# The FFN down projection as seven products instead of eight: one level of Strassen's algorithm in a full-layer kernel

## The chip, the cores and the metric

The kernel runs on one core of one Trainium2 chip. The metric is the device time of one execution in microseconds. The kernel before was run three times: 1833.81, 1831.93 and 1827.96 us, median 1831.93. One further execution was recorded by the hardware profiler; all rows below are from that one. In the text, PE is the matrix engine (PEld its weight loads), DVE the vector engine, ACT the scalar engine, POOL the engine also called GpSimd, and SP the engine that here only issues DMAs.

## The reference

One layer over 1088 tokens (1024 prompt, 64 sample) of width 1024. Attention and an mLSTM branch come first; then the part that this case is about:

```
x = x + g1 * (merged @ w_out)
u2 = _rmsnorm(x, norm2_g) * (1 + sc2) + sh2
x = x + g2 * ((silu(u2 @ w_ff_gate) * (u2 @ w_ff_up)) @ w_ff_down)
y = _rmsnorm(x, final_g)
```

`w_ff_gate` and `w_ff_up` are 1024x2816, `w_ff_down` is 2816x1024, all fp32. The gain `g2` differs between the two groups of tokens. Call the gated product h (2816 features, 22 blocks of 128).

## The kernel before

Everything is feature-major: a tile holds 128 features by tokens, so a residual of width 1024 is 8 blocks of 128x1088. Each fp32 factor is split into a high and a low fp32r part, and one product is three matmuls (`mm3`, lines 76 to 78: high weight by high operand, high by low, low by high) into one PSUM accumulator. The split of a tile is a cast (ACT line 47, or POOL line 53) and a subtraction (DVE line 56, or POOL line 59).

The stages that the change touches, in order of time:

- **Output projection**, up to about 1071 us. The first token half is done block by block, then the second one in the loop `again`, which reloads five of the weight blocks and splits off their low part on POOL (`wl_wp`, line 59). POOL also adds up the squares for the second norm (`acc`, line 1104).
- **Gate and up projections**, about 1071 to 1545 us, in 32 jobs (`jobs`, `gate_up`). They already are a one-level Strassen form: seven products (order 1, 6, 5, 7, 2, 3, 4) on token quarters of 272, 12 matmuls of 128x272 each (line 1363), in four PSUM banks, with DVE and ACT combining the banks. Jobs 0 to 9 do the first ten hidden blocks for token half 0, jobs 10 to 21 do hidden blocks 10 to 21 for both halves, jobs 22 to 31 do the first ten again for half 1. Sums of weight quarters for the first ten blocks are made ahead, during attention, in DRAM (`wsum_d`): POOL issues DRAM-to-DRAM DMAs, a copy (line 172) and one that accumulates (line 170), and each is tied to its moment by a one-element DMA of SP into the same tile (line 166) on which it must wait. For the other twelve blocks POOL adds the weights on chip (`S`, lines 1306 to 1316). Each job ends with a store of its 128x544 piece of h to DRAM (`h_d`, line 1357).
- **Down projection**, from 1545 us on. `ffn_down` takes the hidden blocks in slices 10-13, 14-17, 18-21, 0-3, 4-7. For each slice it goes through the 8 output blocks m and three token chunks (320, 384, 384); a chunk takes 4 hidden blocks x 3 matmuls into one bank (`ps_fd`), and DVE then adds the bank times g2 into the residual accumulator `x1f` (`add_x1`, line 1439). The weights are loaded by SP and split on POOL (`wide_unit`, `wh_fd` and `wl_fd`); h is loaded back and split by ACT and DVE (`load_h`); POOL adds the residual (line 1460).
- **Last slice and final norm.** Hidden blocks 8 and 9 (`ps_fdl`) are done chunk by chunk, and behind each chunk come squares, their sum by matmul (`ps_ssy`), the reciprocal root, transposes (`ps_y`, line 1515) and the store of y.

The order on every engine is the order of the program text, rearranged by a scheduler; engines meet by semaphores. Tiles of a tag rotate through a fixed number of buffers, and a tile can only be written when the readers of its predecessor are done: raw, high and low weights have three buffers each, the pool `up` sixteen of 128x1088.

## Time and profile before

| | |
|---|---|
| median of three runs | 1831.93 us |
| lowest and highest run | 1827.96 and 1833.81 us |
| profiled execution, device time | 1832.56 us |
| its span in the trace | 1830.9 us |
| mean granted PE clock in it | 0.983 |
| PE busy | 1756.2 us, 96% of the span |

The profiled execution is 0.6 us above the median of the runs. About 1.7 us of its device time lie outside of the span of the trace. Times of day in the text (such as "1545 us") count from the start of the span. A row of a group of instructions gives line, engine, operation, output and inputs, shape, count, then busy time and the mean of one in ns, then idle time ahead of the group and who ended it. Matmuls overlap in their pipeline, so the mean of one is longer than the time from one start to the next.

### The profile page before, as it was taken

What the parts mean: (1) busy time and instruction counts of PE and PEld (TensorE: products, weight loads), DVE (VectorE), ACT (ScalarE), POOL (GpSimd) and SP (SyncE); (2) the same over time, 40 slices, a digit from 0 to 9 for tenths busy, and PEclk for the clock granted to TensorE, in tenths of its full rate; (3) what the DMA queues carried; (4) which work ended last, traced back from release to release, by engine and by line L of the source; (5) the groups of instructions that cost most, each with busy time, mean ns of one, the idle gap of its engine ahead of it and who ended that gap; (6) DMA issues with size and microseconds to landing.
All of it is one profiled execution on the core that took longest, in us unless ns stands there. A gap on an engine that the chain in (4) does not pass through costs nothing. (4 is left out here: it accounts for less than half of the span.)

```text
span 1830.9 us, 31719 instructions
## 1 busy us (share of the span) xinstructions
PE 1756.2 (96%) x12388; PEld 1691.3 (92%) x12388; DVE 1001.2 (55%) x1903; ACT 671.6 (37%) x1401; POOL 675.7 (37%) x554
## 2 busy tenths in 40 slices
...
GB/s 275 108 89 209 153 194 152 196 122 143 173 144 142 128 135 148 158 262 140 164 214 195 65 153 176 191 89 72 77 72 80 217 201 204 151 145 109 47 13 98
DMA packets 313208, 265.54 MB, mean 145 GB/s; under 512 B 13670, under 2 KB 285282, under 8 KB 313058
## 3 DMA queue, kind: packets, MB, share of 16 engines
...
q14 instruction: 52, 0.43, 0.1%
...
## 5 line engine op out<-in xcount | busy, mean ns | idle before, releaser
L76 PE MATMUL ps_fd<-hh,wh_fd 128*128 128x384 f32 (+1 forms) x480 | 157.1, 327 | 1.2 <-DVE hst L1355 1.2
L78 PE MATMUL ps_fd<-hh,wl_fd 128*128 128x384 f32 (+1 forms) x480 | 157.2, 327 | 0.0
L77 PE MATMUL ps_fd<-hl,wh_fd 128*128 128x384 f32 (+1 forms) x480 | 157.0, 327 | 0.0
L56 DVE TENSOR_TENSOR w<-wr,w 128x512 fp32r<-128x512 f32 x140 | 95.3, 691 | 38.9 <-ACT w L47 35.8
L1439 DVE SCALAR_TENSOR_TENSOR x1f<-ps_fd,mod,x1f 128x384 f32<-128x384 f32 (+2 forms) x128 | 60.4, 497 | 101.6 <-PE ps_fd L78 101.6
L47 ACT CAST w<-wr 128x512 fp32r<-128x512 f32 x140 | 85.2, 620 | 73.4 <-PE ps_gc L1363 24.7
L390 DVE TENSOR_TENSOR_SCAN re<-re 128x128 f32<-128x128 f32 (+3 forms) x64 | 102.3, 1600 | 15.0 <-ACT re L386 14.7
L53 POOL TENSOR_SCALAR wh_fd<-wr_fd 128x1024 fp32r<-128x1024 f32 x20 | 24.8, 1241 | 227.1 <-PE ps_ga L1363 119.4
L76 PEld LDWEIGHTS ps_fd<-hh,wh_fd 128*128 128x128 f32 x480 | 90.1, 188 | 1.4 <-POOL wl_fd L59 1.4
L78 PEld LDWEIGHTS ps_fd<-hh,wl_fd 128*128 128x128 f32 x480 | 90.1, 188 | 0.0
L77 PEld LDWEIGHTS ps_fd<-hl,wh_fd 128*128 128x128 f32 x480 | 90.1, 188 | 0.0
L47 ACT CAST hh<-hr 128x1088 fp32r<-128x1088 f32 (+1 forms) x26 | 24.0, 962 | 174.9 <-PE ps_fd L77 151.4
L1363 PE MATMUL ps_ga<-b1h,w 128*128 128x272 f32 x352 | 74.5, 291 | 2.9 <-ACT w L47 1.8
L386 ACT ACTIVATE re<-z 128x512 f32<-128x512 f32 (+2 forms) x96 | 47.4, 494 | 80.5 <-DVE z L382 66.0
L1363 PE MATMUL ps_gb<-b6h,w 128*128 128x272 f32 x352 | 75.1, 292 | 0.2 <-ACT g L1348 0.2
L1363 PE MATMUL ps_gd<-b7h,w 128*128 128x272 f32 x352 | 73.9, 289 | 0.0
L1363 PE MATMUL ps_gc<-b5h,w 128*128 128x272 f32 x352 | 73.8, 289 | 0.0
L1363 PE MATMUL ps_ga<-b2h,w 128*128 128x272 f32 x352 | 73.8, 289 | 0.0
L1363 PE MATMUL ps_gc<-b3h,w 128*128 128x272 f32 x352 | 73.7, 288 | 0.0
L1363 PE MATMUL ps_gd<-b4h,w 128*128 128x272 f32 x352 | 73.6, 289 | 0.0
L56 DVE TENSOR_TENSOR al<-ps_a,ah 128x512 fp32r<-128x512 f32 (+1 forms) x80 | 49.4, 629 | 32.0 <-ACT ah L47 31.7
L76 PE MATMUL ps_ga<-uh,wh_ga 128*128 128x384 f32 (+1 forms) x192 | 65.5, 341 | 0.4 <-DVE mod L227 0.4
...
## 6 DMA issues: line engine op xcount, KB each, us to landing
...
```

The source lines that it names most:

```text
L47: nc.scalar.copy(out, in_)
L53: nc.gpsimd.tensor_scalar(out, in_, 1.0, 0.0, ALU.mult, ALU.add)
L56: nc.vector.tensor_sub(out, in_, h.bitcast(F32))
L76: nc.tensor.matmul(ps, wh, xh, start=first, stop=False)
L77: nc.tensor.matmul(ps, wh, xl, start=False, stop=False)
L78: nc.tensor.matmul(ps, wl, xh, start=False, stop=last)
L386: nc.scalar.activation(rest[:, c0 : c0 + w], ps, AF.Sigmoid, scale=-scale)
L390: nc.vector.tensor_tensor_scan(r, r, r, 1.0, ALU.mult, ALU.bypass)
L1363: nc.tensor.matmul(ps, w[:, a, j, :], b[j // 2][:, j % 2, :], start=p in (1, 6, 5, 7) and j == 0 and k == 0, stop=j == 3 and k == 2, skip_ ...
L1439: nc.vector.scalar_tensor_tensor(x1[m][:, lo:hi], ps[:, lo - s : hi - s], mod[:, 40 + m, g : g + 1], x1[m][:, lo:hi], ALU.mult, ALU.add)
```

## The change

The down projection is cut in two along each of its three sides: hidden blocks into 11 even and 11 odd ones, outputs into m 0-3 and m 4-7, tokens into the first quarters of both halves (quarters 0 and 2) and the second ones (1 and 3). With one level of Strassen's algorithm in Winograd's form, seven products take the place of eight. Each product has 11 k-blocks, 4 output blocks and two pieces of 272 tokens, three matmuls each: 1848 matmuls of 128x272 in place of 1584 of 128x384 or 128x320. The order is 1, 2, 6, 5, 3, 7, 4 (`dn_seq`). Each product runs in two parts `mp` of two output blocks, that is in four banks, and the whole contraction stays in PSUM: products 2, 3 and 4 go on in the banks of 1, 5 and 7.

What feeds it:

- Four tables of weight sums in DRAM (`dsum_d`), in 16 steps of 1408 rows x 257 columns, with the same pair of DMAs as `wsum_d`: four in the loop `again`, one in each of jobs 10 to 21.
- Operand sums `tb_d` and `tc_d` (`t_job`): 22 times two loads of a 128x544 piece of h, four DVE additions of 128x272 and two stores, one at product 2 of each half-job from job 10 on while there are any, the last one behind the last job.
- Operands (`dn_operand`): 77 loads of 128x2x272, a cast on ACT and a subtraction on DVE, one `up` buffer for both parts. Weights (`dn_weights`): 14 times three groups of 4, 4 and 3 k-blocks by two output blocks; the cast is on ACT and the subtraction on DVE, so POOL has no part in the down projection any more.
- `x1f` is loaded from DRAM with the residual in it (8 loads of 128x1088). Product 1 is copied to `us` by ACT, product 6 is subtracted from it by DVE and goes to three of the four quarters of the output; the others are added as before.
- The final norm goes by token quarter (`finish`): quarter 1 behind the first part of product 4, quarters 3 and 0 within its second part, quarter 2 at the end.

```diff
+    def tied_sum(dst, edge, src, add, when):
+        nc.sync.dma_start(edge, when)
+        if add:
+            nc.gpsimd.dma_start(dst, src, accum_op=ALU.add)
+        else:
+            nc.gpsimd.dma_start(dst, src)
+    FP = FFB // 2
+    w4 = w_d.rearrange("(k two p) n -> two k p n", two=2, p=P)
+    dsum_d = {x: dram.tile([FP, P, 2, 257], F32, name=f"dsum{x}_d") for x in (1, 2, 3, 4)}
+    dsum_parts = {1: ((0, 512), (1, 512)), 2: ((0, 0), 1), 3: ((0, 0), (0, 512)), 4: ((1, 0), 2)}
+    dsum_todo = [(x, k, c) for x in (1, 2, 3, 4) for k in range(2) for c in range(2)]
+    def dsum_step(when):
+        if dsum_todo:
+            x, k, c = dsum_todo.pop(0)
+            src = dsum_parts[x][k]
+            if isinstance(src, int):
+                src = dsum_d[src][:, :, c, :]
+            else:
+                c0 = src[1] + 255 * c
+                src = w4[src[0], :, :, c0 : c0 + 257]
+            e = 0 if c else 256
+            tied_sum(dsum_d[x][:, :, c, :], dsum_d[x][0, 0:1, c, e : e + 1], src, k, when)
...
         sqs = wo_half(m, 1, ws, m == again[0], m == again[-1], some)
+        if m in again[1::2]:
+            dsum_step(x1v(m, HT, T)[0:1, 0:1])
...
                 nc.sync.dma_start(h_d[i][:, HT * h : HT * (h + 1)], hst)
+                if h == 0 and i >= NF:
+                    dsum_step(hst[0:1, 0:1])
...
+    def t_job(j, h):
+        r = slice(HT * h, HT * (h + 1))
+        b, c = (npl.tile([P, HT], F32, tag=t, name=f"f{t}{j}_{h}", bufs=1) for t in ("rr", "t2"))
+        nc.sync.dma_start(b, h_d[2 * j][:, r])
+        nc.sync.dma_start(c, h_d[2 * j + 1][:, r])
+        b0, b1, c0, c1 = b[:, :QT], b[:, QT:], c[:, :QT], c[:, QT:]
+        nc.vector.tensor_sub(b0, b0, b1)
+        nc.vector.tensor_sub(b1, c1, b1)
+        nc.vector.tensor_add(c1, c1, b0)
+        nc.vector.tensor_sub(c0, c1, c0)
+        nc.sync.dma_start(tb_d[j][:, r], b)
+        nc.sync.dma_start(tc_d[j][:, r], c)
+    dn = {}
+    def quarters(ap):
+        return ap.rearrange("p (h r t) -> p h r t", h=2, r=2)
+    def dn_operand(p, k, raw):
+        src, r = {1: (h_d[2 * k], 0), 2: (h_d[2 * k + 1], 0), 3: (h_d[2 * k + 1], 1), 5: (tb_d[k], 0),
+                  7: (tb_d[k], 1), 4: (tc_d[k], 0), 6: (tc_d[k], 1)}[p]
+        raw = raw.rearrange("p (h t) -> p h t", h=2)
+        oh, ol = (x.rearrange("p (h t) -> p h t", h=2) for x in
+                  (lambda t: (t[:, :HT], t[:, HT:]))(up.tile([P, T], F32R, tag="u", name=f"o{p}_{k}")))
+        nc.sync.dma_start(raw, quarters(src)[:, :, r])
+        hi_act(oh, raw)
+        lo_dve(ol, raw, oh)
+        dn[p, k] = oh, ol
+    dn_order = {p: list(range(FP)) for p in order}
+    dn_order[1] = list(range(NF // 2, FP)) + list(range(NF // 2))
+    def early_operands():
+        for k in dn_order[1]:
+            dn_operand(1, k, mtile(f"hr{k}", F32))
...
-            todo = chain([early_h(b) for b in slices[0]])
+            todo = early_operands()
         def hook(p, last):
             if last and raw:
                 nxt[p] = weight_op(nxt_i, p, raw)
-            if (k < NF and p in (6, 2)) or (k >= FFB and p == 5):
+            if (k < NF and p in (6, 2)) or (k >= FFB and p == 5) or (k == FFB and p == 6):
                 step(todo)
+            if k >= NF and p == 2 and sums_todo:
+                t_job(*sums_todo.pop(0))
...
+        if k >= NF and i % 2:
+            sums_todo += [(i // 2, h) for h in halves]
...
+    for x in sums_todo:
+        t_job(*x)
...
-    def ffn_down(blocks, first):
...
-                for c, (s, e) in enumerate(CHUNKS):
-                    ps = dbank(f"ps_fd{r0}_{m}_{c}")
-                    for j, i in enumerate(blocks):
-                        mm3(ps[:, : e - s], wh[:, j, mi, :], wl[:, j, mi, :], hh[i][:, s:e], hl[i][:, s:e], j == 0, j == nb - 1)
-                    add_x1(m, ps, s, e, first)
...
+    def evac(p, m, h, ps):
+        if p == 1:
+            nc.scalar.copy(us[m][:, h], ps)
+        elif p == 6:
+            nc.vector.tensor_sub(us[m][:, h], us[m][:, h], ps)
+            if h:
+                add_x1(m, None, 1, us[m])
+                add_x1(m + 4, None, 1, us[m])
+                for i in range(2):
+                    add_x1(m + 4, i, 0, us[m][:, i])
+        else:
+            m_, r = {2: (m, 0), 5: (m + 4, 1), 3: (m, 1), 7: (m + 4, 1), 4: (m + 4, 0)}[p]
+            add_x1(m_, h, r, ps)
+            if p == 4:
+                norm_step(m_, r, h)
+            elif p != 5 and h:
+                norm_step(m_, r)
...
+    def dn_weights(p, mp, ks):
+        def fills(raw):
+            raw, x = raw.rearrange("p (k b) n -> p k (b n)", b=2), 0
+            for ks_ in runs(ks):
+                k0, k1 = ks_[0], ks_[-1] + 1
+                if p in (1, 2, 4):
+                    c0 = 256 * mp + (512 if p == 4 else 0)
+                    src = w4[int(p != 1), k0:k1, :, c0 : c0 + 256]
+                else:
+                    src = dsum_d[{6: 2, 5: 1, 3: 4, 7: 3}[p]][k0:k1, :, mp, mp : mp + 256]
+                yield raw[:, x : x + k1 - k0, :], src.rearrange("k p n -> p k n")
+                x += k1 - k0
+        raw = wp.tile([P, KB, P], F32, tag="wr", name=f"wr_d{p}_{mp}_{ks[0]}")
+        for dst, src in fills(raw):
+            nc.sync.dma_start(dst, src)
+        wh, wl = (wp.tile([P, KB, P], F32R, tag=t, name=f"{t}_d{p}_{mp}_{ks[0]}") for t in ("wh", "wl"))
+        n = 2 * len(ks)
+        hi_act(wh[:, :n], raw[:, :n])
+        lo_dve(wl[:, :n], raw[:, :n], wh[:, :n])
+        return [x.rearrange("p (k b) n -> p k b n", b=2) for x in (wh, wl)]
...
+    def dn_mm(p, mp, mi, h, w, j, k):
+        (wh, wl), (oh, ol), ps = w, dn[p, k], banks5[mp, mi, h]
+        ks = dn_order[p]
+        for i, (a, b) in enumerate(((wh, oh), (wh, ol), (wl, oh))):
+            nc.tensor.matmul(ps, a[:, j, mi, :], b[:, h], start=p in (1, 6, 5, 7) and k == ks[0] and i == 0,
+                             stop=k == ks[-1] and i == 2, skip_group_check=True)
...
+    dn_seq = (1, 2, 6, 5, 3, 7, 4)
+    for x, p in enumerate(dn_seq):
+        ks = dn_order[p]
+        groups = [ks[0:4], ks[4:8], ks[8:]]
+        coming = [] if p == 4 else [(dn_seq[x + 1], k) for k in dn_order[dn_seq[x + 1]]]
+        def prepare(n):
+            for p_, k in coming[:n]:
+                dn_operand(p_, k, dn_raw(f"hr{p_}_{k}"))
+            del coming[:n]
+        prepare(16 - FP)
+        for mp in range(2):
+            if p == 1 and mp:
+                for m in range(KB):
+                    nc.sync.dma_start(x1[m], x1_d[m])
+            if p in (1, 6, 5, 7):
+                for h in range(2):
+                    for mi in range(2):
+                        banks5[mp, mi, h] = pbank(mp, f"ps_d{p}_{mp}_{mi}_{h}")[:, :QT]
+            if p < 4 or p > 4:
+                for ks_ in groups:
+                    w = dn_weights(p, mp, ks_)
+                    for j, k in enumerate(ks_):
+                        for mi in range(2):
+                            for h in range(2):
+                                dn_mm(p, mp, mi, h, w, j, k)
+                        if mp:
+                            prepare(1)
+                for mi in range(2):
+                    for h in range(2):
+                        evac(p, 2 * mp + mi, h, banks5[mp, mi, h])
             else:
+                ws = [dn_weights(p, mp, ks_) for ks_ in groups]
+                for h in range(2):
+                    for mis in ((0, 1),) if (mp, h) != (1, 1) else ((0,), (1,)):
+                        for w, ks_ in zip(ws, groups):
+                            for j, k in enumerate(ks_):
+                                for mi in mis:
+                                    dn_mm(p, mp, mi, h, w, j, k)
+                        for mi in mis:
+                            evac(p, 2 * mp + mi, h, banks5[mp, mi, h])
+                    if mp == 0 and h == 1:
+                        finish(1, 0)
+                    elif mp and h == 0:
+                        finish(3, 0)
+                        finish(0, 0)
+    finish(2, 1)```

Where it moves work, three places. **PE at the start of the down projection**, before (`ps_fd` with output block and chunk, `hh` and `hl` the parts of h):

```order
L76 MATMUL ps_fd_0_0_17276<-hh_15934,wh_fd_0_17271 128x320 [waits DVE_49,Pool_49]
L77 MATMUL ps_fd_0_0_17276<-hl_15935,wh_fd_0_17271 128x320
L78 MATMUL ps_fd_0_0_17276<-hh_15934,wl_fd_0_17272 128x320 [waits Pool_49]
L76 MATMUL ps_fd_0_0_17276<-hh_16216,wh_fd_0_17271 128x320
L77 MATMUL ps_fd_0_0_17276<-hl_16217,wh_fd_0_17271 128x320
```

and now (`ps_d` with part, output block in it and token half; `o_5` the operand of k-block 5, both of its parts in one tile):

```order
L1580 MATMUL ps_d_0_0_0_17557<-o_5_16107,wh_d_0_5_17563 128x272 [waits DVE_49,Activation_49]
L1580 MATMUL ps_d_0_0_0_17557<-o_5_16107,wh_d_0_5_17563 128x272
L1580 MATMUL ps_d_0_0_0_17557<-o_5_16107,wl_d_0_5_17564 128x272
L1580 MATMUL ps_d_0_0_1_17559<-o_5_16107,wh_d_0_5_17563 128x272 x2
L1580 MATMUL ps_d_0_0_1_17559<-o_5_16107,wl_d_0_5_17564 128x272
```

One accumulator stays with one bank for all 11 k-blocks, PE goes round four banks per k-block, and it waits for ACT and DVE where it waited for POOL.

**SP between the last job and the second product.** In the kernel before, the last store of h stands behind the weights of the next slices:

```order
L1357 DMA h_d<-hst_1_17007 128x544 [waits DVE_49]
L64 DMA wr_fd_3_17551<-in_w_ff_down 128x4x256 [waits DMAHW3_49,Pool_49]
L64 DMA wr_fd_0_17645<-in_w_ff_down 128x4x256 [waits DMAHW4_49,Pool_49]
L1357 DMA h_d<-hst_1_17132 128x544 [waits DMAHW1_49,DVE_49]
L64 DMA wr_fd_1_17737<-in_w_ff_down 128x4x256 [waits DMAHW5_49,DMAHW2_49,Pool_49]
```

Now, from the last store of h on (`ft` is the second load of the last `t_job`, `hr` the raw operands of product 2):

```order
L1385 DMA h_d<-hst_1_17390 128x544 [waits DVE_49]
L1404 DMA ft_1_17500<-h_d 128x544 [waits DMAHW4_49]
L1425 DMA hr_0_17532<-h_d 128x2x272 [waits DMAHW6_49]
L1425 DMA hr_1_17537<-h_d 128x2x272 [waits DMAHW7_49]
L1425 DMA hr_2_17542<-h_d 128x2x272 [waits DMAHW0_49,PE_49]
```

and the last of them ahead of the weights of product 2:

```order
L1425 DMA hr_10_17838<-h_d 128x2x272 [waits DMAHW2_49,DVE_49]
L1425 DMA hr_0_17913<-tc_d 128x2x272 [waits DMAHW3_49,DVE_49]
L1425 DMA hr_1_17918<-tc_d 128x2x272 [waits DMAHW4_49,DVE_49]
L1564 DMA wr_d_0_0_17938<-in_w_ff_down 128x4x256 [waits DMAHW5_49]
L1564 DMA wr_d_0_4_17992<-in_w_ff_down 128x4x256 [waits DMAHW6_49,DVE_49]
```

In between stand two stores of the `t_job`, eight loads of `x1f` and the other operands of product 2. The weights of product 2 now stand 25 rows behind the last store of h.

**POOL in the jobs with sums on chip.** Before, job 12 and the start of 13:

```order
L1306 TENSOR_TENSOR S_12_13362<-wr_u_13324 128x512 [waits DMAHW3_49]
L1313 TENSOR_TENSOR S_12_13398<-wr_g_13322,wr_u_13324 128x512 [waits DMAHW0_49,DVE_49]
L1307 TENSOR_TENSOR S_12_13363<-S_12_13362,wr_g_13322 128x512 [waits Pool_49]
L1316 TENSOR_TENSOR S_12_13436<-wr_g_13322,S_12_13363 128x512 [waits DVE_49,Pool_49]
L1306 TENSOR_TENSOR S_13_13603<-wr_u_13565 128x512 [waits DMAHW7_49]
```

and now:

```order
L1334 TENSOR_TENSOR S_12_13410<-wr_u_13372 128x512 [waits DMAHW5_49]
L1341 TENSOR_TENSOR S_12_13446<-wr_g_13370,wr_u_13372 128x512 [waits DMAHW6_49,DVE_49]
L1335 TENSOR_TENSOR S_12_13411<-S_12_13410,wr_g_13370 128x512 [waits Pool_49]
L177 DMA dsum_d<-in_w_ff_down 1408x1x257 [waits DMAHW1_49,DMASW5_49]
L1344 TENSOR_TENSOR S_12_13494<-wr_g_13370,S_12_13411 128x512 [waits DVE_49,Pool_49]
```

One DMA of the sums, which waits for SP's one-element DMA, stands ahead of the last weight sum of each such job.

200 lines of the change are left out of this document (73 added, 127 removed).

## The prediction

> **What bounds the kernel now.** I read the page's busy shares and its chain first, then the waits of PE from the output projection on, then the stretches of the last 800 us one by one.
>
> ```profile
> PE 1756.2 (96%) x12388; PEld 1691.3 (92%) x12388; DVE 1001.2 (55%) x1903; ACT 671.6 (37%) x1401; POOL 675.7 (37%) x554
> PE ps_ga L1363 7%; PE ps_gc L1363 7%; PE ps_gd L1363 7%; PE ps_fd L78 4%; PE ps_fd L76 4%; PE ps_fd L77 4%; PE ps_gb L1363 3%; PE ps_fdl L78 0%; PE ps_fdl L76 0%; PE ps_fdl L77 0%; DMA wr<-wsum_d 0%; DVE w L56 0%; DVE y L1524 0%; PE ps_ssy L1132 0%; PE ps_y L1515 0%
> ```
>
> PE is busy for 96%, and the chain's named parts are its matmuls, the down projection's (`ps_fd`) among them. In the part that the change touches, PE waits for next to nothing (waited for: total, times, longest):
>
> ```profile
> PE ps_ga L1363 <- ACT w L47: 1.8, 1, 1.8
> PE ps_fd L76 <- DVE hst L1355: 1.2, 1, 1.2
> PE ps_ga L1363 <- DVE x L1096: 1.1, 1, 1.1
> ```
>
> By stretch (columns: length, busy time of PE, PEld, DVE, ACT, POOL with counts, granted clock, DMA share, GB/s):
>
> ```profile
> 1023.00:1071.00 48.00, 47.43 (x368) 46.91 (x366) 39.80 (x49) 28.71 (x54) 25.03 (x17) 0.97 0.31 97
> 1071.00:1190.00 119.00, 116.48 (x912) 115.73 (x913) 94.92 (x180) 68.94 (x132) 6.87 (x5) 0.99 0.63 181
> 1190.00:1310.00 120.00, 120.00 (x957) 120.00 (x956) 60.77 (x120) 37.01 (x74) 29.81 (x24) 1.00 0.25 77
> 1436.00:1546.00 110.00, 108.84 (x867) 108.65 (x866) 76.19 (x144) 51.52 (x98) 8.99 (x6) 1.00 0.67 196
> 1546.00:1600.00 54.00, 54.00 (x329) 54.00 (x329) 29.96 (x43) 8.54 (x8) 18.88 (x9) 1.00 0.52 179
> 1546.00:1560.00 14.00, 14.00 (x88) 14.00 (x88) 7.91 (x11) 4.00 (x4) 3.64 (x2) 1.00 0.92 340
> 1786.00:1812.00 26.00, 26.00 (x179) 25.92 (x178) 16.25 (x38) 20.75 (x41) 15.33 (x17) 1.00 0.15 61
> 1812.00:1831.00 19.00, 8.90 (x68) 7.70 (x66) 9.74 (x27) 7.34 (x14) 3.40 (x5) 0.82 0.43 153
> ```
>
> From 1546 to 1812 us PE has no gap and its clock is whole: the time of the down projection is the time of its matmuls. So the first question is what a matmul costs, as a start-to-start distance. Three shapes (start, duration; the third with 12 per row):
>
> ```profile
> 1785.74 0.34 PE L78 MATMUL ps_fdl<-hh,wl_fdl 128*128 128x384 f32 x1
> ...
> 1787.86 0.34 PE L78 MATMUL ps_fdl<-hh,wl_fdl 128*128 128x384 f32 x1
> 1804.76 0.31 PE L76 MATMUL ps_fdl<-hh,wh_fdl 128*128 128x320 f32 x1
> ...
> 1805.49 0.31 PE L78 MATMUL ps_fdl<-hh,wl_fdl 128*128 128x320 f32 x1
> 1247.51 1.51 PE ps_gd L1363 x12
> 1249.02 1.51 PE ps_ga L1363 x12
> ```
>
> The first pair is 12 starts apart: 2.12/12 = 0.1767 us for 384 columns. The second is 5 apart: 0.73/5 = 0.146 (0.147 over a longer row of them) for 320. Twelve matmuls of 272 take 1.51: 0.1258. Per column that is 0.460, 0.459 and 0.462 ns, so the price is by columns, with nothing fixed worth naming. The 1190-1310 row confirms it (957 in 120 us: 0.1254).
>
> **The matmuls.** Before, counted from the text: 22 blocks x 8 outputs x 3 passes is 528 per chunk, so 1056 of 384 columns and 528 of 320: 1056 x 0.1767 + 528 x 0.147 = 186.6 + 77.6 = 264.2 us. The first and the last matmul of the stage, and some transposes between them:
>
> ```profile
> 1545.75 0.38 PE L76 MATMUL ps_fd<-hh,wh_fd 128*128 128x320 f32 x1 [1.16 <-DVE hst L1355]
> ...
> 1811.29 2.38 PE L1515 MATMUL ps_y<-ident,x1f 128*128 128x128 f32 x20
> ...
> 1818.23 0.31 PE L78 MATMUL ps_fdl<-hh,wl_fdl 128*128 128x320 f32 x1
> ```
>
> With the last one's own slot PE runs from 1545.8 to 1818.4, 272.6 us; the 8.4 beyond the matmuls are transposes and sums of squares. After: 1848 x 0.1257 = 232.3. A transpose costs 0.11 (2.1 us between the starts of 20); three of four token quarters, 72 transposes, now lie ahead of the last matmul, and some sums: 9. For 14 half products with a change of banks I add 1.5. Sum 242.8, or **29.8 less**.
>
> The Trainium skill, page "TensorE: Matmul & The Clock Gate", section "Back-to-back issue gap", speaks against this: it gives a sustained spacing of about 81 ns at 128 columns and 131 ns at 512 for a stream of weight loads and matmuls, so mostly a price per instruction. Interpolated (an estimate from that page), 272, 320 and 384 columns would cost 99.8, 106 and 114.3 ns, the old stage 176.7 us and the new one 184.4, a loss of 7.7. The trace disagrees: 125.8 against 176.7 ns is a ratio of 1.40, that of the columns 1.41. The trace decides; what such a price would do here by its rows is the first rival.
>
> **The tail.** From 1818.4 to the end of the span (1830.9) are 12.5 us: last addition, square, sums, root, scaling, store. The new tail has the same links for one quarter of 272 tokens instead of 320, without the step that ends POOL's and DVE's `acc`, but four banks instead of six make its last transposes wait for a read-out. I take -0.5 (from -2 to +1).
>
> **Feeding the new stage.** Unit costs by the nearest rows:
>
> ```profile
> L56 DVE TENSOR_TENSOR hl<-hr,hh 128x544 fp32r<-128x544 f32 x8 | 5.6, 721 | 0.6 <-ACT hh L47 0.6
> L47 ACT CAST hh<-hr 128x544 fp32r<-128x544 f32 x8 | 5.0, 644 | 1.7 <-DMA hr<-h_d 1.6
> L1356 DVE SCALAR_TENSOR_TENSOR hst<-hst,g 128x272 f32<-128x272 f32 x35 | 17.0, 486 | 0.4
> L47 ACT CAST wh_wp<-wr_wp 128x1024 fp32r<-128x1024 f32 x5 | 5.2, 1045 | 3.8 <-PE ps_wo L77 3.8
> ```
>
> A half product lasts 132 x 0.1257 = 16.6 us. In it ACT casts 11 x 256 weight columns (2.9 us by the last row) and on average 5.5 operands (3.5): 6.4. DVE subtracts the same (1.35 + 1.35 + 1.0, scaled from 721 ns per 544, and 4.0) and reads out four banks (4 x 0.49): 9.7. In product 6's read-out DVE has four subtractions and the additions of three quarters, about 7.5, so 15.2 of 16.6. SP moves 1.44 MB of weights and 1.5 MB of operands: 2.9 MB in 16.6 us are 177 GB/s, against 340 at a share of 0.92 in the 1546-1560 row. Three buffers let a group of weights be made two groups (10 to 12 us) ahead of its use. All of it fits beside PE: nothing, with a bound of 2.5 us per half product if DVE came late each time.
>
> **Transition: +2 (0 to 5).** Product 2's weights stand behind about 10 MB (product 2's operands 3.1, `x1f` 4.5, the rest stores, sums and these weights). SP can first issue them when the last store of h has landed, some 4.5 us after the last job; at the 340/0.92 = 370 GB/s that a full queue moves they arrive at about 31 us, with cast and subtraction 33; needed at 33.2. A tie, so I take 2.
>
> **Operand sums: +1 (0 to 6).** 88 DVE additions of about 0.44 to 0.49 us and 88 transfers of 272 KB. In jobs 10 to 21 DVE has 60.8 of 120 us, so 15 of the 22 lie there free. Seven remain for the last ten jobs (110 us): 7 x 4 x 0.45 = 13 us on DVE (76 of 110 before, less the old early slices), and SP waits in each for a store to land, a load, and DVE; behind it stand the next job's weights, which now arrive about a job ahead.
>
> **Weight sums: +2 (0 to 6).** The nearest rows are the sums of the other weights (minimum, median, maximum of an issue on POOL in ns; POOL's wait for the tie; time to landing):
>
> ```profile
> L170 POOL DMA_DIRECT2D wsum_d<-wsum_d x4: 1038/1060/1081, 262.5 to 373.2; - x4
> POOL wsum_d L170 <- DMA wsum_d<-cvo: 22.5, 4, 6.1
> DMA to landing us min/median/max: 9.4/10.8/14.6
> L59 POOL TENSOR_TENSOR wl_wp<-wr_wp,wh_wp 128x1024 fp32r<-128x1024 f32 x5 | 13.0, 2603 | 24.5 <-ACT wh_wp L47 24.5
> 262.00:285.00 23.00, 23.00 (x152) 23.00 (x151) 14.08 (x18) 6.95 (x14) 12.41 (x10) 1.00 0.86 173
> ```
>
> The new ones have 1408 rows instead of 512: an issue costs 1.1 us if it is by DMA, 2.9 if by row. In jobs 10 to 21 one stands ahead of a single weight sum that is needed half a job later: nothing; the cover is gone if the issue and its tie take over 7 us. The DMAs of these jobs (253 us: 24 half-jobs of 84 matmuls) come near a share of 0.9: 0.25 as in the 1190-1310 row, 12 x 10.8 us at 0.86 (0.44), and 15 operand sums of 1.1 MB at 370 GB/s (0.18). In `again` four issues with ties (2 to 6 us each) stand ahead of `wl_wp` blocks of 2.6 us, in a loop of 6 us per block where POOL is 25 of 48 busy: one or two may come late for PE, and first-job weights behind them. Two microseconds.
>
> **Sum:** 1832.6 - 29.8 - 0.5 + 2 + 1 + 2 = **1807.3**, so 1807 (25 under the median of the runs).
>
> **Rivals.** *A price per matmul.* If the mean durations (336 ns for 384 columns, 309, and 290 for 272) were what PE pays:
>
> ```profile
> L76 PE MATMUL ps_fd<-hh,wh_fd 128*128 128x384 f32 x320 | 107.6, 336 | 0.0
> L76 PE MATMUL ps_fd<-hh,wh_fd 128*128 128x320 f32 x160 | 49.4, 309 | 1.2 <-DVE hst L1355 1.2
> L1363 PE MATMUL ps_ga<-b1h,w 128*128 128x272 f32 x352 | 74.5, 291 | 2.9 <-ACT w L47 1.8
> ```
>
> 1848 x 0.290 against 1056 x 0.336 + 528 x 0.309 is 536 against 518: 18 slower, with the added terms 1855. The starts speak against it. *Preparation eats it.* If the sums keep the DMA engines near the 0.86 row through jobs 10 to 31, SP's loads come late by a microsecond each job, twice in the last ten: 12 + 20 with the terms above leaves about 1832, no change. For it: the last ten jobs already run at 0.67; against: weights come a job ahead and PE waits 1.8 us in all. *The new stage is bound by its feed* (the slower side): DVE makes the low part of every weight and operand and reads out every bank in order; where a half product's queue exceeds the 10 to 12 us of lead, PE stops, and the next half product starts with the debt. At 2.5 us for each of 14, 35: 1842. It decides once DVE's part goes from 9.7 over 16.6; only product 6 comes near.
>
> **How the numbers follow.** The forecast with its bounds (1800 with no added cost and the short tail, 1822 with all added costs near their upper ends) has 0.82; preparation eats it 0.09 (1822 to 1836); feed 0.06; price per matmul 0.03. Range 1800 to 1826. A measurement of this kernel tells about 0.3%, 5.5 us, from no change. Faster: 0.82 and 0.03 of the second case, 0.85; the same 0.06 of it; slower 0.09.
>
> **What would show it.** Right: matmuls of 128x272 in `ps_d` with 12 in 1.51 us; the stretch from the first `ps_d` to the last about 243 us with PE busy throughout but a gap below 5 us 33 us after its start; POOL empty in it. Wrong: waits of PE for ACT or DVE weights (`wl_d`) at each half product (feed), waits for `w` of DMA in jobs 22 to 31 or for `wl_wp` in the output projection (preparation), or starts farther apart than 0.126 (price). If the down stage starts over 10 us later than 1545.8, my terms for the sums were wrong.

## The result, and the profile after

The kernel got slower: 1901.59 us (four runs, 1896.52 to 1905.75) against 1832.87 (four runs, 1827.96 to 1836.01), a ratio of 1.0376 with a 95% interval of 1.0341 to 1.0411. I had forecast 1807, so 95 us were missing. The profiled execution took 1902.57 us, 1900.8 in its span, 69.9 more than before. Of ten runs of the kernel `onchip_spread4` further down one took 2865 us, at a granted clock of 0.633; it is left out of that kernel's ratio.

From the page of the kernel after: the busy shares, the chain by engine, and one of its costliest groups.

```profile
PE 1756.0 (92%) x12670; PEld 1682.2 (88%) x12670; DVE 1050.3 (55%) x2002; ACT 734.7 (39%) x1504; POOL 581.5 (31%) x497
...
PE 11%; DMA 2%; DVE 0%; ACT 0%; issue 0%; SPq 0%; DVEq 0%; ACTq 0%
...
L1393 PE MATMUL ps_gc<-b3h,w 128*128 128x272 f32 x352 | 81.5, 310 | 35.8 <-DVE hst L1371 35.7
```

PE is as busy as before in microseconds (1756.0 against 1756.2) although the down projection is shorter, and the gate and up matmuls of one bank (`ps_gc`) have 35.8 us of idle time ahead of them. In the kernel before, PE was idle for 3.7 us in that whole stage. Now the stretches of the kernel after, with the same columns as in the prediction: length, busy time of PE, PEld, DVE, ACT and POOL with counts, granted clock, DMA share, GB/s.

```profile
1071.00:1190.00 119.00, 103.36 (x757) 99.98 (x756) 78.94 (x154) 57.42 (x111) 6.80 (x6) 0.94 0.80 200
1190.00:1310.00 120.00, 108.39 (x813) 106.69 (x812) 71.93 (x137) 35.43 (x74) 32.00 (x23) 0.94 0.64 171
1310.00:1436.00 126.00, 106.00 (x787) 104.89 (x786) 62.84 (x122) 29.04 (x60) 33.30 (x24) 0.92 0.72 168
1436.00:1546.00 110.00, 100.42 (x756) 99.34 (x756) 63.50 (x125) 37.46 (x74) 17.14 (x13) 0.95 0.81 206
1546.00:1647.00 101.00, 88.08 (x673) 86.94 (x671) 65.90 (x134) 42.37 (x83) 0.00 (x0) 0.95 0.75 221
...
1647.00:1680.00 33.00, 32.89 (x253) 32.92 (x254) 13.15 (x19) 11.62 (x19) 0.00 (x0) 0.95 0.93 325
1680.00:1889.00 209.00, 207.84 (x1677) 206.79 (x1677) 125.26 (x218) 96.84 (x145) 0.00 (x0) 1.00 0.54 163
```

The down projection starts at 1647.1 instead of 1545.75 us, 101.3 late, and then does what was forecast: from there to 1889.8 us, 242.7 in all, PE has hardly a gap. Nearly all of the loss lies in the gate and up stage, whose first matmul starts 5.4 us late (1076.99 instead of 1071.55 us). From 1071 to 1647 us PE is idle for 576 - 506.3 = 69.7 us, against 3.7 in the same stage before, and its 3786 matmuls cost 506.3/3786 = 0.1337 us each against 0.1260, at a granted clock of 0.92 to 0.95 instead of 1.00. That is 66 us of gaps and 29 of slower matmuls; the remaining 6 are 46 matmuls more in the stretch, the end of the output projection, whose last matmul starts at 1076.36 instead of 1070.14 us.

Who holds PE, and who holds those? The longest waits of the kernel after in that stage and at its end (waited for: total, times, longest), for PE, then DVE, SP's queue and POOL (`frr` and `ft` are the two tiles that a `t_job` loads):

```profile
PE ps_gc L1393 <- DVE hst L1371: 35.7, 11, 9.9
PE ps_gd L1393 <- DVE hst L1373: 8.9, 3, 4.6
PE ps_ga L1393 <- ACT p L1366: 7.7, 3, 4.9
PE ps_d L1580 <- DVE hst L1383: 7.6, 1, 7.6
...
DVE frr L1406 <- DMA frr<-h_d: 66.7, 17, 11.3
DVE frr L1407 <- DMA ft<-h_d: 47.6, 19, 7.6
...
SPq L1404 <- DMA h_d<-hst: 57.8, 19, 11.1
SPq L1410 <- DVE frr L1407: 42.7, 15, 4.1
...
POOL dsum_d L175 <- DMA dsum_d<-hst: 41.7, 4, 20.0
```

Lines 1403 to 1411 are `t_job`. PE waits for bank read-outs (lines 1371 and 1373), which are short additions; DVE comes late to them because, in its order, a `t_job` stands ahead and waits for its two loads. SP stands in the same `t_job` (for a store of h to land before it loads that h back, and for DVE before it stores a sum), and behind it stand weight loads of the next job. And POOL waits for the tie of a weight sum. One stall shows the links, from the timeline of the kernel after (start, duration, engine, line, operation; in brackets the idle time before it and who ended it):

```profile
1407.95 1.91 POOL L175 DMA_DIRECT2D dsum_d<-in_w_ff_down  x1
...
1417.97 0.32 SPq L1403 DMA_DIRECT2D frr<-h_d  x1
...
1417.17 0.43 DVE L1369 TENSOR_TENSOR u<-p,ps_gb 128x272 f32<-128x272 f32 x1
1428.91 1.18 DVE L1406 TENSOR_TENSOR frr<-frr 128x272 f32<-128x272 f32 x1 [11.30 <-DMA frr<-h_d]
1430.02 0.43 DVE L1371 TENSOR_TENSOR hst<-ps_gc,u 128x272 f32<-128x272 f32 x1
...
1430.50 0.60 PE L1393 MATMUL ps_gc<-b3h,w 128*128 128x272 f32 x1 [9.87 <-DVE hst L1371]
1430.89 0.43 PE L1393 MATMUL ps_gc<-b3l,w 128*128 128x272 f32 x1
...
1433.16 0.43 PE L1393 MATMUL ps_gc<-b3h,w 128*128 128x272 f32 x1
```

POOL issues a weight sum at 1408. While it runs, SP issues a load of 272 KB that takes 10.9 us. DVE stands idle for 11.3 us; the read-out is behind that addition in its order and takes 0.43 us, and PE has waited 9.87 us for it. Then PE is slow as well: ten matmuls start in 1433.16 - 1430.89 = 2.27 us, 0.227 each instead of 0.1257. The Trainium skill, page "TensorE: Matmul & The Clock Gate", section "HAM oscillation — how this bites in real kernels", says that an idle stretch of PE beyond some 3.4 us brings its clock down and that the next work starts cold; the trace agrees, with a spacing 1.8 times the usual one behind this gap of 9.87 us. The granted clock is 0.50 from 1430.5 to 1435 us. The trace also shows that short gaps cost only themselves: of the gaps in this stage the seven of 3.8 to 9.9 us are each followed by ten matmuls 0.227 us apart or more, and the thirteen of 0.4 to 2.7 us by ten that are 0.125 to 0.127 apart; two of 3.4 and 3.7 us have slow and usual ones behind them. (One gap of 2.05 us in the kernel `no_wsums` below was followed by slow ones, though.)

How long that weight sum took, and what it cost the DMA engines, stands in the DMA view of the kernel after for 1400 to 1434 us (queue, packets, MB, share of the 16 engines; then the issue, its size, time to landing). q1 are SP's transfers, q0 POOL's:

```profile
q1 hardware_dynamic: 4181, 3.69, 38.0%
q0 software_dynamic: 2227, 1.61, 33.2%
...
dsum_d<-in_w_ff_down POOLq DMA_DIRECT2D x1, 1413.5 KB, 22.2
```

It landed after 22.2 us, and a MB of it takes 20.6% of the engines' time in the stretch where a MB of SP's loads and stores takes 10.3%.

### The profile page after: what moved, and what is told of

It reads as the page before. It is cut to its first block, busy times and chain, and to the rows that moved or that the text cites. A ratio compares the mean times of both kernels' runs of the same rounds, so it can differ in the third digit from the quotient of the medians.

```text
span 1900.8 us, 32728 instructions
## 1 busy us (share of the span) xinstructions
PE 1756.0 (92%) x12670; PEld 1682.2 (88%) x12670; DVE 1050.3 (55%) x2002; ACT 734.7 (39%) x1504; POOL 581.5 (31%) x497
## 3 DMA queue, kind: packets, MB, share of 16 engines
q1 hardware_dynamic: 340290, 267.03, 48.1%
q0 software_dynamic: 30208, 62.04, 15.9%
## 5 line engine op out<-in xcount | busy, mean ns | idle before, releaser
L1580 PE MATMUL ps_d<-o,wh_d 128*128 128x272 f32 x1232 | 232.6, 288 | 8.7 <-DVE hst L1383 7.6
L1580 PEld LDWEIGHTS ps_d<-o,wh_d 128*128 128x128 f32 x1232 | 194.1, 189 | 9.1 <-ACT g L1380 7.7
L1580 PE MATMUL ps_d<-o,wl_d 128*128 128x272 f32 x616 | 177.5, 289 | 0.0
L47 ACT CAST w<-wr 128x512 fp32r<-128x512 f32 x140 | 83.5, 618 | 91.0 <-DMA wr<-wsum_d 27.6
L1580 PEld LDWEIGHTS ps_d<-o,wl_d 128*128 128x128 f32 x616 | 116.3, 189 | 0.2 <-DVE wl_d L56 0.2
L1393 PE MATMUL ps_gc<-b3h,w 128*128 128x272 f32 x352 | 81.5, 310 | 35.8 <-DVE hst L1371 35.7
L1393 PEld LDWEIGHTS ps_gc<-b3h,w 128*128 128x128 f32 x352 | 63.0, 204 | 38.7 <-DVE hst L1371 38.6
L1393 PE MATMUL ps_gd<-b4h,w 128*128 128x272 f32 x352 | 81.6, 311 | 8.9 <-DVE hst L1373 8.9
L1393 PE MATMUL ps_ga<-b2h,w 128*128 128x272 f32 x352 | 75.6, 293 | 7.7 <-ACT p L1366 7.7
L1393 PE MATMUL ps_ga<-b1h,w 128*128 128x272 f32 x352 | 77.3, 296 | 2.4 <-ACT g L1376 2.1
L56 DVE TENSOR_TENSOR wl_d<-wr_d,wh_d 128x1024 fp32r<-128x1024 f32 (+1 forms) x42 | 47.6, 1135 | 54.4 <-ACT wh_d L47 53.9
L1393 PE MATMUL ps_gb<-b6h,w 128*128 128x272 f32 x352 | 75.4, 291 | 1.9 <-ACT w L47 1.8
L1393 PE MATMUL ps_gd<-b7h,w 128*128 128x272 f32 x352 | 75.3, 293 | 1.4 <-DVE hst L1383 1.4
L1393 PE MATMUL ps_gc<-b5h,w 128*128 128x272 f32 x352 | 74.6, 291 | 2.0 <-DVE g L1379 1.6
L47 ACT CAST o<-hr 128x544 fp32r<-128x544 f32 x77 | 49.5, 645 | 62.2 <-DMA hr<-h_d 44.3
L1393 PEld LDWEIGHTS ps_gd<-b4h,w 128*128 128x128 f32 x352 | 64.7, 210 | 9.8 <-DVE hst L1373 5.0
L47 ACT CAST wh_d<-wr_d 128x1024 fp32r<-128x1024 f32 (+1 forms) x42 | 41.1, 979 | 78.7 <-PE ps_d L1580 69.6
L56 DVE TENSOR_TENSOR o<-hr,o 128x544 fp32r<-128x544 f32 x77 | 54.4, 724 | 30.7 <-ACT o L47 30.2
L1393 PEld LDWEIGHTS ps_ga<-b2h,w 128*128 128x128 f32 x352 | 59.0, 191 | 8.7 <-ACT p L1366 8.4
## 6 DMA issues: line engine op xcount, KB each, us to landing
dsum_d<-in_w_ff_down POOLq DMA_DIRECT2D x12, 1413.5 KB, 13.7
```

Source lines behind the costliest of these rows:

```text
L47: nc.scalar.copy(out, in_)
L56: nc.vector.tensor_sub(out, in_, h.bitcast(F32))
L1393: nc.tensor.matmul(ps, w[:, a, j, :], b[j // 2][:, j % 2, :], start=p in (1, 6, 5, 7) and j == 0 and k == 0, stop=j == 3 and k == 2, skip_ ...
L1580: nc.tensor.matmul(ps, a[:, j, mi, :], b[:, h], start=p in (1, 6, 5, 7) and k == ks[0] and i == 0, stop=k == ks[-1] and i == 2, skip_group ...
```

## The experiments

All times are set beside a kernel before of 1832.7 to 1835.4 us, measured in the same batch. Since the loss builds up in the gate and up stage, one table follows it through all kernels: how many us later than in the kernel before a half-job begins (the start of ACT's copy of its first bank; second job, job 10, job 22), and how much later the down projection does. A kernel that leaves work out is marked with *. The times are single runs, or medians of four where a ratio is given (ten for `onchip_spread4`); the lags are from the one profiled execution of each kernel.

| kernel | job 1 | job 10 | job 22 | down | time, us |
|---|---|---|---|---|---|
| after | 23.2 | 29.5 | 75.9 | 101.3 | 1901.59 |
| neither * | 0.2 | -0.3 | -0.3 | -0.4 | 1797.66 |
| no_opsums * | 17.5 | 17.4 | 22.4 | 30.7 | 1828.84 |
| no_wsums * | -0.7 | 7.0 | 12.6 | 35.9 | 1837.68 |
| pool_adds | 17.2 | 28.5 | 73.0 | 95.6 | 1896.93 |
| early | 92.8 | 99.4 | 107.3 | 128.3 | 1931.32 |
| early_poolq | 92.4 | 93.2 | 95.1 | 100.5 | 1902.53 |
| early_keep | 96.3 | 95.3 | 95.9 | 99.9 | 1898.43 |
| keep | 21.6 | 22.5 | 63.9 | 80.9 | 1881.32 |
| spread4 | 14.9 | 15.3 | 57.0 | 72.4 | 1869.43 |
| spread8 | 26.8 | 26.6 | 60.7 | 62.8 | 1864.91 |
| onchip | 29.0 | 28.7 | 40.5 | 52.1 | 1851.73 |
| onchip16 | 10.4 | 10.5 | 51.8 | 62.3 | 1859.63 |
| onchip_no_wsums * | 1.6 | 2.4 | 7.8 | 9.4 | 1808.88 |
| onchip8 | 3.4 | 4.0 | 53.7 | 55.7 | 1857.40 |
| onchip_half * | 2.5 | 2.9 | 17.7 | 19.9 | 1819.30 |
| onchip_spread4 | 10.2 | 10.8 | 21.9 | 33.5 | 1835.76 |

A lag can be there before anything that was added runs. The first matmul of the output projection starts at 950.68 us in the kernel before, at 954.08 in `after`, 948.16 in `no_opsums`, 953.29 in `keep`, 959.56 in `onchip` and 958.25 in `onchip16`, and none of these has an added instruction ahead of it. So a lag, and the time of a single run, can be off by up to about 10 us; what a stage adds to the lag is the safer number.

### One half of the preparation at a time

Two causes were to be told apart first: waits for the loads of `t_job` in the order of an engine (theory A), and DMA engines filled by the weight sums (theory B). `no_opsums` takes out the operand sums, `no_wsums` the weight sums, `neither` both:

```diff
# no_opsums, neither
     def t_job(j, h):
+        return
...
-        src, r = {..., 5: (tb_d[k], 0), 7: (tb_d[k], 1), 4: (tc_d[k], 0), 6: (tc_d[k], 1)}[p]
+        src, r = {..., 5: (h_d[2 * k], 0), 7: (h_d[2 * k], 1), 4: (h_d[2 * k + 1], 0), 6: (h_d[2 * k + 1], 1)}[p]
# no_wsums, neither
-        if dsum_todo:
+        if False:
...
-                    src = dsum_d[{6: 2, 5: 1, 3: 4, 7: 3}[p]][k0:k1, :, mp, mp : mp + 256]
+                    src = w4[0, k0:k1, :, 256 * mp : 256 * mp + 256]
```

> The 22 operand sums (loads, DVE additions, stores) are left out; products 5, 7, 4 and 6 read h itself in the place of the sums, so their operands are not the right ones, but every transfer and matmul of the down projection stays. In the changed kernel the lag behind the kernel before grows by 22 us up to the first job's end, by 12 in jobs 1 to 9, by 44 in jobs 10 to 21 and by 23 in jobs 22 to 31, and the down projection itself takes the 242 us forecast. Theory A (DVE works in order and waits for the loads of the operand sums, ahead of the bank read-outs that PE waits for): the 79 us of jobs 1 to 31 go, the first 22 stay, about 1823 us (1815 to 1835). Theory B (the weight sums crowd the DMA engines, everything else comes late): little changes, over 1875 us.

> The 16 steps of weight sums are left out; products 6, 5, 3 and 7 load a quarter of the weights themselves in the place of a sum, so the result is not the reference's, but the loads of the down projection are as many and as large. Theory A: only the 22 us up to the first job go (four steps stand in the output projection there), and loads land a little earlier, about 1870 us (1855 to 1882). Theory B: DMA engines are free, the waits for the operand sums' loads shrink to nothing, about 1825 us (1805 to 1840).

> Both the weight sums and the operand sums are left out (operands and weights of the dependent products are read from h and from the weights themselves, so the result is not the reference's). Both theories: what is left is the new down projection on its own, 1832.6 - 30.3 + 2 = 1804 us (1800 to 1810), with the down stage at 242 to 244 us. If the time is over 1820, a third cause lies in the down stage's transition.

With neither, 1797.66: the new down stage by itself gains 35 us, and no half-job is late. The weight sums alone bring that to 1828.84 (31 more), the operand sums alone to 1837.68 (40 more), both to 1901.59 (104 more). So either alone eats the gain, and 33 us come only from the two together (27, if what each kernel had lost or won before its output projection is taken off). The first run came out as theory A had it, the second as theory B, so neither theory holds alone. The table says where the two meet: between jobs 10 and 22 the weight sums alone add 5 us to the lag, the operand sums alone 6, and both together 46. Two stretches of `neither`, one in jobs 10 to 21 and one at the start of the down stage:

```profile
1190.00:1310.00 120.00, 120.00 (x957) 120.00 (x956) 60.50 (x119) 37.30 (x74) 30.04 (x24) 1.00 0.25 77
...
1546.00:1680.00 134.00, 134.00 (x1079) 134.00 (x1078) 81.21 (x124) 60.95 (x89) 0.00 (x0) 1.00 0.74 236
```

The gate and up stage is as before, to the count of its matmuls, and the new stage runs without a gap at 134/1079 = 0.1242 us per matmul.

What the weight sums do alone: in `no_opsums` 16 of the 31 us are lost between the first job and the second. Its stretch of 1085 to 1105 us, and ACT's waits around it:

```profile
1085.00:1105.00 20.00, 14.01 (x95) 13.27 (x93) 10.13 (x20) 5.80 (x11) 0.00 (x0) 0.91 1.01 196
```

```profile
ACT w L47 <- DMA wr<-in_w_ff_up: 9.4, 1, 9.4
ACT w L47 <- DMA wr<-wsum_d: 8.1, 4, 3.5
```

The DMA engines are full (1.01), and ACT waits for the first jobs' weights: the four steps of the loop `again` run while these are loaded. After that the single steps of jobs 10 to 21 cost 5 us, and the last ten jobs 8.

What the operand sums do alone: in `no_wsums` they cost 8 us in the first ten jobs, 6 in jobs 10 to 21 and 23 in the last ten. DVE's waits for the loads, and PE's for the read-out of line 1371, in `no_wsums`:

```profile
DVE frr L1407 <- DMA ft<-h_d: 58.6, 20, 7.9
DVE frr L1406 <- DMA frr<-h_d: 45.4, 18, 5.3
...
PE ps_gc L1393 <- DVE hst L1371: 3.6, 4, 1.3
```

DVE waits 104 us in all, hardly less than the 114 of the kernel after, but no wait is longer than 7.9 us where the longest there was 11.3, and PE waits 3.6 us for that read-out where it waited 35.7. So the sum of DVE's waits does not tell what they cost; with the weight sums beside them the single waits got longer, and PE ran dry.

### Which engine's order

`pool_adds` moves the 88 additions to POOL, so that DVE no longer waits for the loads:

```diff
-        nc.vector.tensor_sub(b0, b0, b1)
+        nc.gpsimd.tensor_sub(b0, b0, b1)
   (and the three additions behind it)
```

> The 88 additions of the operand sums are done by POOL instead of DVE; all transfers are as in the changed kernel. Theory A: DVE no longer waits for these loads, POOL does; PE's waits for the bank read-outs on DVE (46 us in the changed kernel) go, some come back through the weight sums of jobs 10 to 21 that POOL makes on chip behind them; about 1855 us (1830 to 1875). Theory B: the same transfers are as late as before, 1890 to 1910 us.

1896.93: no gain to speak of, and within what theory B expected. The waits of `pool_adds`, of SP, ACT and PE:

```profile
SPq L1404 <- DMA h_d<-hst: 68.4, 20, 6.7
SPq L1410 <- POOL frr L1407: 63.3, 21, 4.3
...
ACT w L47 <- POOL S L1344: 73.5, 11, 15.6
...
PE ps_ga L1393 <- ACT p L1366: 26.2, 8, 8.6
```

The stall has moved, not gone. Now POOL waits for the same loads ahead of its weight sums `S`, ACT waits for those (73.5 us), and PE for ACT. That DVE alone was the cause is refuted. The waits fit a wider reading, that it matters little which engine on the way to PE waits in its order for a load that comes late; this run doesn't part that from theory B.

The next three move all 16 weight-sum steps into the attention stage, where earlier sums of this kind already are; `early_poolq` also puts the loads, additions and stores of `t_job` on POOL's queue, and `early_keep` takes most of the operand sums from tiles that are still on chip:

```diff
# early: one step behind each of 16 units of attention
-        if m in again[1::2]:
-            dsum_step(x1v(m, HT, T)[0:1, 0:1])
...
-                if h == 0 and i >= NF:
-                    dsum_step(hst[0:1, 0:1])
...
+                fill += [ads[x], dsum_unit(16 + ai - na + x)]
# early_poolq: the same, and in t_job nc.vector and nc.sync -> nc.gpsimd
# early_keep: the same, and for half 1 and all of blocks 10 to 21, in short:
-        nc.sync.dma_start(c, h_d[2 * j + 1][:, r])
+        b = kept_h[2 * j] if j < NF // 2 else even[h]   # c is hst itself, even[h] is loaded
```

> All 16 steps of weight sums are moved into the attention stage (one behind each of 16 units of its filler work); nothing else changes. Without these steps the changed kernel took 1837.7 us. Theory C (what costs time is SP's order: an issue that waits for a store to land or for DVE holds up every later load and store, and the DRAM-to-DRAM sums lengthen each landing) and theory D (the volume of all transfers together crowds the DMA engines) both say 1838 to 1848: the 31 us of the weight sums and the 33 that both together cost go, the 40 of the operand sums stay.

> As the run with early weight sums, and the operand sums are wholly POOL's: it issues their 88 transfers on its own queue and does the 88 additions. The transfers are as many and as large. Theory C: SP and DVE no longer wait for any of it; what is left is POOL being late with the weight sums of jobs 10 to 21, 1800 to 1818 us. Theory D: as many bytes at the same times, 1835 to 1850 us.

> As the run with early weight sums, and the operand sums are made at the end of each odd job: its own h is taken from the tile on chip, the even block's is loaded at the start of the odd job (jobs 10 to 21, stored long before) or also taken from the chip (jobs 22 to 31); five pairs of the first ten blocks are still loaded both, in even jobs. 61 transfers of 272 KB instead of 88, and no load waits for a store just issued. Theory C: 1799 to 1810 us, faster than the kernel before by 1.2 to 1.8%. Theory D: 30% fewer bytes give 30% of the 40 us back, about 1828 us.

`early` took 1931.32, `early_poolq` 1902.53 and `early_keep` 1898.43 (ratio 1.0346, 1.0328 to 1.0364), all three far outside what I expected, and for a reason that I had not priced: the attention stage has no room either. Two stretches there, of `early` and of the kernel before:

```profile
600.00:700.00 100.00, 69.77 (x491) 63.80 (x489) 45.75 (x88) 31.20 (x73) 26.22 (x27) 0.86 0.86 184
700.00:800.00 100.00, 66.62 (x437) 59.60 (x427) 45.59 (x90) 27.55 (x65) 24.25 (x22) 0.81 0.83 174
```

```profile
600.00:700.00 100.00, 94.66 (x673) 85.81 (x672) 66.89 (x132) 45.26 (x106) 25.74 (x28) 0.97 0.59 144
700.00:800.00 100.00, 91.96 (x685) 81.86 (x683) 77.12 (x151) 47.00 (x110) 39.99 (x42) 0.98 0.66 170
```

The DMA share goes from 0.59 and 0.66 to 0.86 and 0.83, and about a third of PE's matmuls in these stretches is pushed out (928 where there were 1358). The first gate and up job is 91 us late.

But these three tell something else apart. Once the jobs run, what do the operand sums cost with no weight sum beside them? From the first job (lags of 91.3, 90.9 and 94.8 us) to the down projection `early` grows later by 37 us, `early_poolq` by 9.6, `early_keep` by 5.1. `early` and `early_poolq` move the same bytes in the same stage, only in another queue; so in that stage, and with no weight sum beside them, it is the order on SP and DVE that costs 27 us, not the volume.

### Operand sums from tiles on chip

`keep` is the change with only the operand sums of `early_keep`; `spread4` and `spread8` also put four or eight of the weight-sum steps into attention, and the rest singly into jobs 10 to 21 or 10 to 17:

```diff
# spread4; spread8: (18, 21, 24, 27, 30, 32, 34, 36) and range(10, 18)
-        if m in again[1::2]:
-            dsum_step(x1v(m, HT, T)[0:1, 0:1])
...
-                if h == 0 and i >= NF:
+                if h == 0 and i in range(10, 22):
...
+                fill += ads[x : x + 1] + [dsum_unit(n)] * (n in (20, 25, 30, 36))
```

> The changed kernel with only the operand sums rearranged: made at the end of each odd job from its tile on chip, the even block's piece loaded early or also taken from the chip. The weight sums are where the change has them. Theory C (SP's and DVE's order; the weight sums lengthen the landings on which they wait): with the waits gone, what both cost together beyond each alone (33 us) and most of the 40 go; the weight sums' own 31 and some 4 stay: 1797.7 + 35 = 1833 us (1826 to 1842). If the two only compete for the DMA engines (theory D), 1850 to 1880.

> As the run before it, and the four weight-sum steps of the output projection are moved into the attention stage, far apart (one per 60 to 100 us); the twelve others stay in jobs 10 to 21. With weight sums alone the lag was 16 us at the first job, nothing up to job 24 and 13 from there on; the first 16 should go: 1797.7 + 4 + 13 + 2 = 1817 us (1805 to 1825), faster than the kernel before by 0.5 to 1.5%.

> As the last, with eight steps in the attention stage (one per 35 to 45 us) and eight in jobs 10 to 17. If the 13 us around jobs 22 to 25 came from the last steps running into the next stage's loads, they go too. If the attention stage has no room for more transfers (16 steps at one per 19 us cost 95 us there), it loses 5 to 25 us instead. 1797.7 + 4 + 5 to 25: 1807 to 1827, I take 1814.

Measured 1881.32, 1869.43 and 1864.91 (the last two are 1.0189 and 1.0173 times the kernel before, with intervals of 1.017 to 1.0207 and 1.0128 to 1.0218). Each gains, all three far less than I expected. In `keep` the loads that are left are where the time goes: pairs of the first ten blocks (line 1432) and the even ones of the other twelve (line 1369). DVE's waits in `keep`:

```profile
DVE frr L1432 <- DMA frr<-h_d: 35.8, 4, 11.5
...
DVE frr L1369 <- DMA frr<-h_d: 22.1, 9, 9.1
```

Thirteen waits of DVE for such a load, still 57.9 us, and four of them alone 9 us each, where the change had 17 of 3.9: taking most of the loads away left some that still lie beside a weight sum, and DVE waits longer for those.

`onchip` leaves no load in the operand sums: h stays in quarter tiles until its partner is there.

```diff
-        nc.sync.dma_start(b, h_d[2 * j][:, r])
-        nc.sync.dma_start(c, h_d[2 * j + 1][:, r])
+        (b0, b1), (c0, c1) = kept_h[2 * j, h], kept_h[2 * j + 1, h]
...
-        hst = gp.tile([P, HT], F32, tag="hst", name=f"hst{i}_{h}", bufs=2)
+        if i >= NF and i % 2 == 0:
+            hst, h0, h1 = None, quarter(f"h0_{i}_{h}"), quarter(f"h1_{i}_{h}")
# onchip16: no step in the loop again; a second one in four jobs
-                if h == 0 and i >= NF:
+                if i >= NF and (h == 0 or i in (10, 13, 16, 19)):
# onchip_no_wsums: onchip with the edit of no_wsums
```

> The changed kernel with all 22 operand sums made from tiles on chip (the even block's h of jobs 10 to 21 is kept in four quarter tiles of the output projection that are free by then), so that none of their 44 loads is left; additions on DVE and stores by SP stay, the weight sums stay where the change has them. In the run that kept only part of them on chip, the lag still jumped by 6 to 11 us at each of the four loaded pairs, where DVE waited 9 us for a load behind a weight sum. Theory A with C (in-order waits of DVE and SP for loads that a weight sum in flight makes late): no such load is left, so the weight sums' own cost remains, as without operand sums: 1829 to 1835 us. If additions and stores themselves cost (DVE time, DMA volume): 1845 to 1865.

> As the last, and the four weight-sum steps of the output projection go into jobs 10, 13, 16 and 19 (a second step in each), so that all 16 stand in jobs 10 to 21, where weight sums alone had cost nothing up to job 17. The 16 us of the first job go; the 13 around jobs 17 to 22 may stay or grow, since the last steps end as late as before: 1797.7 + 2 + 5 to 15 = 1805 to 1815 us, taken 1810, faster than the kernel before by 1.0 to 1.5%.

> The operand sums made on chip as in the last two runs, and no weight sums (the dependent products load a quarter of the weights themselves, so the result is not the reference's). It parts what is left of the operand sums (88 additions on DVE, 44 stores of 272 KB by SP and POOL-free) from the weight sums. Theory A with C: the loads' waits were the cost, so 1798 to 1804 us against 1837.7 with the loads. If additions and stores cost by themselves: 1810 to 1830.

`onchip_no_wsums` took 1808.88: without loads the operand sums cost 11 us instead of 40, and the lag at the marks of the table is never more than 10 us. That lies between the two ranges, so additions and stores do cost something by themselves. With the weight sums as in the change, `onchip` took 1851.73, over the first range and inside the second. But 9 us of its lag were there before the output projection; without them its down projection starts 43 us late, where `onchip_no_wsums`, taken likewise, has 8 and `no_opsums` 33. So with the loads gone the two halves nearly just add up: between jobs 10 and 22 the 12 single steps and the operand sums cost 12 us together, 5 of them without any weight sum, where they cost 41 in `keep`. The interaction of the two halves came with the loads. The run takes the loads' bytes away along with the waits for them, so it doesn't tell by itself how much was the waiting; the shift of the waits in `pool_adds`, and `early` against `early_poolq`, speak for it. What was left was 20 us in the output projection and the first job, from the four steps of `again` (as much as in `no_opsums`), and 12 in the last ten jobs. `onchip16` moved those four steps into jobs 10, 13, 16 and 19, where a second step follows in the other half of the job, and came out no better (1859.63; ratio 1.0127, 1.0099 to 1.0154): 10 at job 10, 8 of them from before the output projection, but 41 lost by job 22, where single steps had cost 12.

### Fewer or better placed weight sums

`onchip8` makes eight sums of whole rows (2.8 MB each) instead of sixteen of half rows, one per job from 10 to 17; `onchip_half` keeps only the eight half-row steps for two of the four tables; `onchip_spread4` is `onchip` with the placing of `spread4`:

```diff
# onchip8
-    dsum_todo = [(x, k, c) for x in (1, 2, 3, 4) for k in range(2) for c in range(2)]
+    dsum_todo = [(x, k) for x in (1, 2, 3, 4) for k in range(2)]
...
+            nc.gpsimd.dma_start(t[:, :, 0:512], src, accum_op=ALU.add)   # second steps, three of the tables
# onchip_half
-        if dsum_todo:
+        if len(dsum_todo) > 8:
```

> All outputs are the reference's. The operand sums on chip, and the weight sums in 8 steps of whole rows (514 or 512 columns) in the place of 16 of 257, one per job from job 10 to 17, none in the output projection. Theory E (a weight sum is free while it is the only large transfer of a job whose weights come a job ahead; it costs where loads are needed soon, in the output projection with the first jobs behind it, in the attention stage and in jobs 18 to 22): 1797.7 + 5 for the operand sums + 0 to 6 = 1803 to 1810 us, faster than the kernel before by 1.2 to 1.6%. If the bytes cost wherever they run (the same 46 MB as before), 1825 to 1850.

> Operand sums on chip; of the weight sums only the eight tied steps for tables 1 and 2 are made, one per job in jobs 10 to 17, none in the output projection and none after job 17; products 3 and 7 read tables 2 and 1 in the place of 4 and 3, so the result is not the reference's. Theory E (a single step per job there is hidden, since the weights come a job ahead and POOL is not held up): as without weight sums, 1808.9 us (1806 to 1814). If every step costs its share of DMA time (some 43 us for 16): 1825 to 1832.

> All outputs are the reference's. Operand sums on chip; four weight-sum steps far apart in the attention stage, where four cost 13 us before, and twelve single ones in jobs 10 to 21, where the last four cost 8. Theory E adds up by place: 1808.9 + 13 + 0 + 8 = 1830 us (1823 to 1836), level with the kernel before. If the cost goes by the number of steps wherever they are, 1850 to 1860 as in the three versions that have 16 steps elsewhere.

`onchip8`: 1857.40 (ratio 1.0127, 1.01 to 1.0153), with 50 us lost between jobs 10 and 22. Its waits, of POOL and of ACT, name a wait of its own making:

```profile
POOL dsum_d L201 <- issue: 36.2, 2, 18.4
POOL dsum_d L201 <- DMA dsum_d<-in_w_ff_down: 18.9, 1, 18.9
```

```profile
ACT w L47 <- POOL S L1337: 56.7, 9, 13.3
```

Without a tie the second sum into a table follows the first one on POOL's queue, and POOL stands there some 18 us (until the first has landed, by the second row; the first row names no releaser), ahead of the weight sums `S` that ACT needs. So this run, 47 us over its forecast range, says nothing on larger transfers.

`onchip_half`: 1819.30, 10 us over no weight sums at all, all of it between jobs 10 and 22; that is between the two ranges, so a step there is not free, as theory E had it, and costs less than its share of DMA time. `onchip_spread4`: 1835.76, as expected, the median of ten runs, nine of which lie between 1828.86 and 1840.52. The ratio is 1.0001 (0.9983 to 1.0019): level with the kernel before. Its last two stretches of the gate and up stage:

```profile
1310.00:1436.00 126.00, 122.62 (x961) 122.17 (x960) 74.99 (x143) 34.97 (x72) 41.03 (x29) 0.99 0.69 165
1436.00:1579.00 143.00, 134.63 (x1037) 132.03 (x1035) 96.72 (x198) 64.26 (x125) 2.81 (x2) 0.99 0.84 228
```

PE is back at 97% of the first and 94% of the second, at a clock of 0.99. Its 33.5 us at the start of the down projection are 10 up to the first jobs (the steps in attention, and some 2 us that were there earlier), 11 from jobs 10 to 21 and 12 from the last ten jobs, and they equal about what the new stage gains. No complete version came out ahead of the kernel before.

## Why the prediction was wrong, step by step

**Matmuls, -29.8: right.** The stage took 242.7 us for a forecast of 242.8, by the price per column. That it agrees so closely is luck: in `neither`, without stalls, its first and last matmul are 239.4 us apart (1545.3 to 1784.8), so the gain was put 3 us too small, and in the kernel after some waits and a granted clock of 0.95 at the start of the stage used up those 3. The first rival's price of 0.290 is refuted by the 0.1242 us per matmul of `neither`. The spacing of the Trainium skill (page "TensorE: Matmul & The Clock Gate", section "Back-to-back issue gap"), interpolated to 99.8 ns for 272 columns, isn't met either: the trace has 124.2.

**Tail, -0.5: right**, from 1889.8 to 1900.8, 11.0 instead of 12.5. **Transition, +2: right.** PE waits once for product 2's weights, 1.2 us (`ps_d` for ACT's `wh_d`). (The 7.6 us ahead of the first `ps_d` come with the operand sums: in `no_opsums` and `neither` they are 1.4 and 1.1.) **Feed, nothing: right**; from 1680 to 1889 us PE is busy for 207.84 of 209, and the third rival never showed. The down stage alone came to -35.0 (1797.66 against 1832.68 in the same batch), where these terms gave -28.3.

**Operand sums, +1 (0 to 6): failed.** They cost 40 us alone, 23 of them in the last ten jobs. For jobs 10 to 21 the reading that they are free was nearly right (6 us), as long as no weight sum ran beside them; that the two meet there was not in the sum. I had read that "SP waits in each for a store to land, a load, and DVE" and what stands behind it, and gave it no price, since DVE had free time (60.8 of 120 us). Free time was the wrong measure: DVE does not spend those 114 us (66.7 and 47.6) working, it waits, and where a wait outlasts PE's lead the read-out behind it comes late for PE. I costed the additions and not the wait in front of them. I asked what is queued behind a wait for SP alone; asked of DVE, it leads to line 1371. I also took the sums to sit in jobs 10 to 31; the scheduler had four of them run from 1124 us on, before job 10.

**Weight sums, +2 (0 to 6): failed.** They cost 31 us alone, 16 of them by the second job, and some 30 more with the other sums. My cover was POOL's time up to the next `S`, with a limit of 7 us for an issue and its tie. The issues were as bounded (1.1 to 1.9 us); the ties were not (41.7 us in four of them, since SP comes late with them; no run takes the ties alone apart). The price that the runs do show was elsewhere: in the loads of others. I had worked out that the DMAs would come near a share of 0.9 in those jobs and then drew nothing from it. The queues of the two pages, of the kernel after and of `neither`:

```profile
q1 hardware_dynamic: 340290, 267.03, 48.1%
q0 software_dynamic: 30208, 62.04, 15.9%
```

```profile
q1 hardware_dynamic: 327586, 242.52, 46.1%
q0 software_dynamic: 12032, 38.84, 9.6%
```

POOL's queue takes 0.159 x 1900.8 - 0.096 x 1796.0 = 130 us more of all 16 DMA engines, 8.1 per step, and SP's 86 us more. The gate and up stage before has about 475 us with shares of 0.63, 0.25, 0.31 (its third stretch) and 0.67, 218 us in all: with these 216, if all of them fell in it, it would be 91% full at its old length. This is an estimate from two kernels and doesn't show which load came late; that loads did is seen in the 10.9 us of the stall above.

**The rival that happened** is "preparation eats it". Its mechanism, loads that come late once the DMA engines are kept near 0.86, is seen in `no_opsums` at 1085 to 1105 us (a share of 1.01), though there in the first jobs, where the rival did not look for it. Its size was off threefold (32 us, against 104; with my other terms those 32 come to 1834 at least, not the 1832 that I wrote), since it had SP's loads late by a microsecond a job, and neither DVE's and SP's own waits nor the lost clock. I gave it 0.09, on the evidence that PE waited 1.8 us in all. That showed how the stage stood without the new load, not what slack it had.

**What stays open.** Why a single step in jobs 10 to 21 costs anything from 0 to 5 us in one kernel and more in another; what makes one execution reach the output projection up to 10 us later than another with nothing added ahead of it; how the interaction of the two halves parts between waits in order and sheer volume; and which load or wait is the late one in the last ten jobs of `onchip_spread4`.
